# A decoder layer in split fp32: stick-breaking heads started apart, their block sums added before the product, and the first loads and table products spaced out

## The chip, the cores and the metric

The kernel runs on one core of one Trainium2 chip. The metric is the device time of one execution in microseconds (us). The kernel before took 1091.46 us, the median of 3 runs (1091.45 to 1092.46). The profile shows another, single execution, whose own time was 1093.85 us; its instructions span 1092.1 us.

In the profile PE is TensorE's matmul stream, PEld its weight loads, DVE is VectorE, ACT is ScalarE, POOL is GpSimd, and SP is the engine that issues most of the loads.

## What is computed

One layer of a decoder for 512 tokens of width 1024, all in fp32. Its first half is a mixer with three kinds of attention that share one input projection; its second half is an MLP. The part that the change touches most is the stick-breaking attention, 8 heads of width 64:

```
z        = q @ k.T * scale
log_keep = where(s < t, log_sigmoid(-z), 0)          # = -softplus(z)
later    = reverse_cumsum(log_keep, over keys) - log_keep
a        = where(s < t, exp(log_sigmoid(z) + later), 0)
o        = a @ v
```

So the weight of key s for query t needs the sum of softplus(z) over all keys between s and t. The other parts are: differential attention (4 heads, with a bias by distance), dilated attention (12 heads in 3 groups, with a bias by distance), a gated merge and an output projection, a layer norm, then `x <- LN(alpha * x + MLP(x) + sigmoid(x Wg) * (p Wp))`.

## The kernel before

**Split fp32.** An fp32 product is made of three products of rounded halves: a value is cast to a rounded type (`h`, on ACT as a rule), the rest is `lo = x - h` (on DVE), and PE sums `h*h`, `h*lo` and `lo*h` in one PSUM bank. Weights go the same way: a load (512 KB, queue SP) into one of 4 `raw` buffers, an ACT cast to `wh` (L223), a DVE subtraction to `wl` (L224), then the matmuls. A projection item is 24 matmuls of 128 x 512. Where a value is -1 or 0 in the other factor (a matrix of ones or a triangle), two products are enough, one with `h` and one with `lo`.

**Items and steps.** The program is a list of items: two projections together at the start (`first_item`, whose 8 pieces of x and 5 pieces of weights have loads of their own), then one projection or one 128-token piece of V each, then the branch products, the output projection and the MLP. The main loop (from L1280) takes items in order. For each it splits weights ahead (`pump`, L229), evacuates the item before from its PSUM bank (two `mm` banks take turns), calls `step()` and issues the matmuls, with another `step()` in the middle. Attention runs as generators that `step()` (L1261) advances: in `waiting` stand 8 stick-breaking heads, 4 dilated heads and 16 blocks of differential attention. A stick-breaking head counts for 3 PSUM banks of 8, so two run at a time; it is advanced at every second step. The next in line starts when the banks allow it and at least `GAP` = 1 step has gone by. So heads 0 and 1 start one step apart, and later pairs as the pair before ends.

**What the order is.** The text order gives priorities. A scheduler then writes one fixed instruction list for each engine, and an engine works through its list in order. Most tiles come from one pool of 42 SBUF buffers of 128 x 512 fp32 (`slot`, L74); a tile can be written only when a buffer is free. A second pool holds 6 PSUM banks (`at_bank`). `tc.issue_after(i)` puts instructions behind `i` on their own engine.

**A stick-breaking head** (`sb_head`, L968). The keys are 4 blocks of 128, and block kb is needed for the queries from kb on: 512, 384, 256 and 256 columns. Blocks 2 and 3 share a bank (`bi` = 2), blocks 1 and 0 have one each. First come q.k products and masks; then per bank the softplus (three ACT passes, one DVE pass, L991 to L994) into `e`, and its split into `sph` (DVE cast, L997) and `spl` (DVE, L998). Then per key block, from the last to the first, a product with a triangle (`tri_r`, L1008) adds the sum inside the block, and for every later block a product with ones (`ones_r`, L1011) adds that block's whole sum, each twice for `sph` and `spl`. After that come exp, split, and the product with V.

**Tables.** The distance biases come from a one-hot matrix: `tables()` (L899), called at item 13, loads it (three DMAs of the POOL queue), makes five products with the bias table (`rel_vec`, L871, 33 rows by 4 columns), copies each on ACT (L873), writes it to DRAM and reads it back shifted (POOL queue, L882). `turn_tables()` at item 21 reverses them with 8 DVE copies (L892). The dilated heads use them first.

**The start.** Nine matmuls on zeros (L831) run while the first loads come in. `fill()` (L169) issues all loads it can, the first 17 in a fixed order on SP: x piece 0, weights 0, x piece 1, weights 1, x 2, x 3, weights 2 and so on.

**The end.** Output rows are finished 128 at a time. `plain` (L699) adds the last products for `tt` = 0 to 3. For `tt` < 3 the norm is `layer_norm_act` (L463): sums on ACT, a power on POOL (L474), two scaling passes (L476) and two finishing passes (L478) on DVE, then the stores. The last rows come in three pieces with statistics on DVE (L742, L743) and `last_norm` (L752).

## Time and profile before

| | before |
|---|---|
| median of 3 runs | 1091.46 us |
| the profiled execution, its own time | 1093.85 us |
| its span of instructions | 1092.1 us |
| PE busy, share of the span | 99% |
| DVE busy | 62% |
| ACT busy | 44% |
| granted PE clock, mean | 0.997 |
| data moved by DMA | 105.71 MB, 97 GB/s |

A row of the timeline has the start in us from the span's start, the duration in us, the engine, the line, the operation, output <- inputs, the shape, and in square brackets how long the engine had been idle before and what ended that. Matmuls overlap: a row's duration is longer than the distance to the next start, and the distance is what a matmul costs in a dense stream. A row of the groups has the count, the busy time, the mean in ns, then the idle time before and its causes. A row of the windows has, for one stretch, the length and each engine's busy us with the number of instructions, then the granted PE clock, the DMA share and GB/s.

### The profile page before, as it was taken

The numbers are of one execution on the slowest core, as the hardware profiler recorded it, in microseconds if no ns is written. First come the engines' busy times: TensorE is split into PE (matmuls) and PEld (weight loads), VectorE is DVE, ScalarE is ACT, GpSimd is POOL, SyncE is SP. The second block draws the span as 40 slices with busy tenths as digits, with TensorE's granted clock in tenths as the row PEclk, the third lists the DMA queues.
The fourth block names the chain that finished last, engine by engine and source line by source line (L and its number), as shares of the span: only waits on it lengthen the run. The fifth ranks groups of instructions, "written<-read, shape, count | busy, mean of one in ns | idle before, by whom it ended". The sixth has DMA issues, their size and how long they took to land.

```text
span 1092.1 us, 13135 instructions
## 1 busy us (share of the span) xinstructions
PE 1078.9 (99%) x5039; PEld 901.4 (83%) x5039; DVE 674.6 (62%) x1197; ACT 478.4 (44%) x795; POOL 31.0 (3%) x55
## 2 busy tenths in 40 slices
PE   9999999999999999999999999999999999999997
PEld 6788788999888888888888888888888888888885
DVE  5878366564343757665444453875686686687676
ACT  6756354443232546455332331333554454454441
POOL 0000200000000000000000020110000000000000
PEclk9999999999999999999999999999999999999999
DMA  7422421120322113122232253243222422322302
GB/s 250 127 97 85 136 78 58 59 97 21 117 89 83 59 39 107 68 78 87 87 97 101 93 182 127 77 166 108 93 97 78 135 97 77 135 97 79 134 1 77
DMA packets 32431, 105.71 MB, mean 97 GB/s; under 512 B 4378, under 2 KB 5290, under 8 KB 32368
## 3 DMA queue, kind: packets, MB, share of 16 engines
q1 hardware_dynamic: 29424, 96.91, 26.2%
q0 software_dynamic: 2368, 7.05, 2.0%
q8 instruction: 39, 0.64, 0.2%
q10 hardware_dynamic: 576, 0.92, 0.2%
q14 instruction: 24, 0.20, 0.1%
HBM read 102.74 MB, written 2.12 MB: 96 GB/s over the span
## 4 chain that ended last, share of the span: by engine, by line
PE 95%; DVE 3%; DMA 1%; ACT 1%; issue 0%; SPq 0%; POOL 0%; DVEq 0%; ACTq 0%
PE mm L87 17%; PE mm L88 17%; PE mm L89 17%; PE mm L333 3%; PE mm L335 3%; PE mm L334 3%; PE mm L672 2%; PE mm L674 2%; PE mm L673 2%; PE at L672 2%; PE at L674 2%; PE at L673 2%; PE mm L567 1%; PE mm L503 1%; PE mm L501 1%; PE mm L568 1%
## 5 line engine op out<-in xcount | busy, mean ns | idle before, releaser
L223 ACT CAST wh<-raw 128x1024 fp32r<-128x1024 f32 (+1 forms) x173 | 178.3, 1031 | 288.7 <-PE mm L88 229.4
L224 DVE TENSOR_TENSOR wl<-raw,wh 128x1024 fp32r<-128x1024 f32 (+1 forms) x173 | 206.2, 1197 | 123.5 <-ACT wh L223 119.7
L87 PE MATMUL mm<-xhT,wh 128*128 128x512 f32 x496 | 196.5, 396 | 0.0
L89 PE MATMUL mm<-xhT,wl 128*128 128x512 f32 x496 | 194.7, 393 | 0.0
L88 PE MATMUL mm<-xlT,wh 128*128 128x512 f32 x496 | 194.5, 392 | 0.0
L89 PEld LDWEIGHTS mm<-xhT,wl 128*128 128x128 f32 x496 | 93.6, 189 | 19.6
L88 PEld LDWEIGHTS mm<-xlT,wh 128*128 128x128 f32 x496 | 93.6, 189 | 18.3 <-issue 0.4
L87 PEld LDWEIGHTS mm<-xhT,wh 128*128 128x128 f32 x496 | 93.5, 189 | 18.2
L87 PE MATMUL mm<-x1hT,wh 128*128 128x512 f32 x256 | 99.6, 389 | 0.0
L88 PE MATMUL mm<-x1lT,wh 128*128 128x512 f32 x256 | 99.6, 389 | 0.0
L89 PE MATMUL mm<-x1hT,wl 128*128 128x512 f32 x256 | 99.6, 389 | 0.0
L333 PE MATMUL mm<-wh,xhT 128*128 128x512 f32 x160 | 65.6, 410 | 0.6 <-DVE sb_kb L108 0.6
L335 PE MATMUL mm<-wh,xlT 128*128 128x512 f32 x160 | 63.1, 394 | 0.0
L334 PE MATMUL mm<-wl,xhT 128*128 128x512 f32 x160 | 63.0, 394 | 0.0
L89 PEld LDWEIGHTS mm<-x1hT,wl 128*128 128x128 f32 x256 | 48.1, 188 | 10.0
L88 PEld LDWEIGHTS mm<-x1lT,wh 128*128 128x128 f32 x256 | 48.1, 188 | 10.0
L87 PEld LDWEIGHTS mm<-x1hT,wh 128*128 128x128 f32 x256 | 48.1, 188 | 9.9
L223 ACT CAST wh<-wsum 128x1024 fp32r<-128x1024 f32 x28 | 29.5, 1055 | 52.5 <-PE mm L88 49.3
L224 DVE TENSOR_TENSOR wl<-wsum,wh 128x1024 fp32r<-128x1024 f32 x28 | 34.2, 1222 | 24.2 <-ACT wh L223 23.6
L333 PEld LDWEIGHTS mm<-wh,xhT 128*128 128x128 f32 x160 | 38.0, 237 | 4.2 <-issue 0.8
L335 PEld LDWEIGHTS mm<-wh,xlT 128*128 128x128 f32 x160 | 38.0, 237 | 3.9
L334 PEld LDWEIGHTS mm<-wl,xhT 128*128 128x128 f32 x160 | 38.2, 239 | 3.3
(336 smaller groups left out, 1972.7 us busy)
## 6 DMA issues: line engine op xcount, KB each, us to landing
raw<-in_wt_dram SPq DMA_DIRECT2D x62, 512.0 KB, 3.3
raw<-in_wu_dram SPq DMA_DIRECT2D x32, 512.0 KB, 3.3
raw<-in_wd_dram SPq DMA_DIRECT2D x32, 512.0 KB, 3.3
raw<-in_wv_dram SPq DMA_DIRECT2D x20, 512.0 KB, 3.3
raw<-in_wb_dram SPq DMA_DIRECT2D x8, 512.0 KB, 3.4
raw<-in_wo_dram SPq DMA_DIRECT2D x8, 512.0 KB, 3.7
raw<-in_wg_dram SPq DMA_DIRECT2D x8, 512.0 KB, 4.2
rawx<-in_xT_dram SPq DMA_DIRECT2D x8, 256.0 KB, 6.0
```

Of the source, the lines that this page charges most:

```text
L87: nc.tensor.matmul(ps, wh, xh, start=start, stop=False, skip_group_check=True)
L88: nc.tensor.matmul(ps, wh, xl, start=False, stop=False, skip_group_check=True)
L89: nc.tensor.matmul(ps, wl, xh, start=False, stop=stop, skip_group_check=True)
L223: nc.scalar.copy(h, raw)
L224: i = nc.vector.tensor_sub(lo, raw, h.bitcast(F32))
L333: nc.tensor.matmul(ps, x1, c["h"][:, s], start=k == 0, stop=False)
L334: nc.tensor.matmul(ps, x1, c["l"][:, s], start=False, stop=False)
L335: nc.tensor.matmul(ps, x2, c["h"][:, s], start=False, stop=k == 7)
L501: nc.tensor.matmul(ps, h[:, q], c["h"][:, s], start=k == 0, stop=False)
L672: nc.tensor.matmul(ps, h[:, q], c["h"][:, s], start=go, stop=False, skip_group_check=True)
L673: nc.tensor.matmul(ps, h[:, q], c["l"][:, s], start=False, stop=False, skip_group_check=True)
L674: nc.tensor.matmul(ps, lo[:, q], c["h"][:, s], start=False, stop=end, skip_group_check=True)
```

## The change

There are five edits and a small one.

1. **Sums ahead of the split.** In `sb_head`, after the softplus of bank 2 DVE adds the two key blocks' `e` (256 columns) into `sm`, ACT casts it and DVE subtracts (a split of 256 columns). After that of bank 1 DVE adds `sm` to `e` in place, and ACT and DVE split that (384 columns). Each of key blocks 2, 1 and 0 then gets one pair of products with ones, from these summed halves, in place of a pair for every later block.
2. **Heads apart.** `GAP` becomes `gap`, 7 steps (3.5 items) until at most 20 generators wait, which is when the 8 stick-breaking heads have started, and 1 after that.
3. **First loads.** `fill()` issues only 4 loads until the first cast of x is in the program, and load 4 (x piece 2) waits on SP for that cast to be done.
4. **One-hot products.** `rel_vec` and `tables` become generators: each step issues one product with its copy and its store, and the shifted loads come in the step after the last. `turn_tables()` moves from item 21 to 22.
5. **The third norm's end.** `layer_norm_act` returns its two finishing passes as a function. For `tt` = 2 they are issued behind the first addition of the last rows (L742).
6. `pump` may split two chunks, where it was one, at items 0, 1 and 2.

```diff
--- before.py
+++ after.py
@@ -140,9 +140,9 @@
 
 
         RING, RAW, NSUM = 7, 4, 3
-        ORDERED = 17
+        ORDERED, AHEAD = 17, 4
         loads, sums, chunks, placed = [], [], [], []
-        st = {"dma": 0, "sum": 0, "split": 0}
+        st = {"dma": 0, "sum": 0, "split": 0, "most": 4}
 
         def load(src, w, own=False):
             s = {"src": src, "w": w, "uses": 0, "own": own}
@@ -167,7 +167,7 @@
             return chunk_of(load(src, w))
 
         def fill():
-            while st["dma"] < len(loads):
+            while st["dma"] < min(len(loads), st["most"]):
                 s = loads[st["dma"]]
                 if not s["own"]:
                     if len(placed) >= RAW and placed[-RAW]["uses"]:
@@ -184,6 +184,10 @@
                 else:
                     i = nc.sync.dma_start(s["raw"], s["src"])
                 st["load"] = getattr(i, "ins", i)
+                if st["dma"] == AHEAD:
+
+                    tc.add_manual_dep(st["load"], st["cast"].name, mybir.DependencyInfo(
+                        mybir.DependencyClass.Sync, mybir.DependencyReason.DATA), reason="first loads alone")
                 st["dma"] += 1
                 add()
             add()
@@ -220,7 +224,9 @@
                 parts = c["dst"]
             for h, lo, a0, a1 in parts:
                 raw = c["from"]["raw"][:, a0:a1]
-                nc.scalar.copy(h, raw)
+                cast = nc.scalar.copy(h, raw)
+                if st["split"] == 0:
+                    st["cast"], st["most"] = getattr(cast, "ins", cast), 1 << 30
                 i = nc.vector.tensor_sub(lo, raw, h.bitcast(F32))
                 st["low"] = getattr(i, "ins", i)
             c["from"]["uses"] -= 1
@@ -474,9 +480,12 @@
             nc.gpsimd.tensor_tensor(r, r, mhalf, OP.pow)
             for h in range(2):
                 nc.vector.scalar_tensor_tensor(ts[h], ts[h], nmu, lnc[g][h], op0=OP.add, op1=OP.mult)
-            for h in range(2):
-                nc.vector.scalar_tensor_tensor(ts[h], ts[h], r, lnc[b][h], op0=OP.mult, op1=OP.add)
-                fin(h, ts[h])
+
+            def rest():
+                for h in range(2):
+                    nc.vector.scalar_tensor_tensor(ts[h], ts[h], r, lnc[b][h], op0=OP.mult, op1=OP.add)
+                    fin(h, ts[h])
+            return rest
 
         xn = {}
 
@@ -698,7 +707,7 @@
 
             def plain(cs, c2, c3, c4):
 
-                sums = {}
+                sums, held = {}, []
                 s6 = slot("bn6e")[:, :18].rearrange("p (a b) -> p a b", b=6)
 
                 ends = [(0, slice(0, 512)), (1, slice(0, 256)), (1, slice(256, 512))]
@@ -737,9 +746,16 @@
                                 def fin(h, y):
                                     (nc.sync if h else nc.scalar).dma_start(
                                         out[0, tt * P:tt * P + P, 512 * h:512 * h + 512], y)
-                                layer_norm_act([acc[tt, 0], acc[tt, 1]], sums[tt], "ln2_g", "ln2_b", fin)
+                                rest = layer_norm_act([acc[tt, 0], acc[tt, 1]], sums[tt], "ln2_g", "ln2_b", fin)
+                                if tt == 2:
+                                    held.append(rest)
+                                else:
+                                    rest()
                             return
-                        nc.vector.tensor_add(t[:, cc], t[:, cc], ps[:, :n])
+                        i = nc.vector.tensor_add(t[:, cc], t[:, cc], ps[:, :n])
+                        if held:
+                            with tc.issue_after(getattr(i, "ins", i)):
+                                held.pop()()
                         nc.vector.bn_stats(s6[:, ends.index((half, cc)), :], t[:, cc])
                         if (half, cc) == ends[2]:
                             last_norm()
@@ -872,6 +888,7 @@
                 sb = slot("rvs")[0:4, :]
                 nc.scalar.copy(sb[:, :n], ps[0:4, :n])
                 nc.gpsimd.dma_start(rv[cols, d0:d0 + n], sb[:, :n])
+                yield
 
         def shifted(h0, n, m):
             ts = []
@@ -903,10 +920,10 @@
             nc.gpsimd.dma_start(oh[0][:33, :], ohd[:, 0:512])
             nc.gpsimd.dma_start(oh[1][:33, :], ohd[:, 512:1024])
             nc.gpsimd.dma_start(oh[2][:33, :], ohd[:, 1024:1536])
-            rel_vec(slice(0, 4), [(oh[0][:33, :], 0, 512), (oh[1][:33, 0:128], 512, 128)])
-            rel_vec(slice(4, 8), [(oh[1][:33, 128:512], 0, 384)])
-            rel_vec(slice(8, 12), [(oh[2][:33, 0:256], 0, 256)])
-            rel_vec(slice(12, 16), [(oh[2][:33, 256:512], 0, 256)])
+            yield from rel_vec(slice(0, 4), [(oh[0][:33, :], 0, 512), (oh[1][:33, 0:128], 512, 128)])
+            yield from rel_vec(slice(4, 8), [(oh[1][:33, 128:512], 0, 384)])
+            yield from rel_vec(slice(8, 12), [(oh[2][:33, 0:256], 0, 256)])
+            yield from rel_vec(slice(12, 16), [(oh[2][:33, 256:512], 0, 256)])
             tab_g0 = shifted(4, 4, 256)
             tab_g1 = shifted(8, 4, 128)
             tab_g2 = shifted(12, 4, 128)
@@ -983,7 +1000,7 @@
                     nc.tensor.matmul(ps[:, 0:P], identb, mask_b[:, 1, :], start=False, stop=False,
                                      skip_group_check=True)
             w = [512, 384, 512]
-            sph, spl = {}, {}
+            sph, spl, later = {}, {}, {}
             for bi in (2, 1, 0):
                 n = w[bi]
                 ps = bank[bi][:, :n]
@@ -1000,16 +1017,33 @@
 
                     tie[:] = [getattr(i, "ins", i) for i in (ln, low)]
                 sph[bi], spl[bi] = h, lo
+
+                if bi == 2:
+                    later[2] = (256, (h[:, HC], lo[:, HC]))
+                    sm = slot("sm")[:, HB]
+                    nc.vector.tensor_add(sm, e[:, HB], e[:, HC])
+                    hl = slot("smp", F32R)
+                    nc.scalar.copy(hl[:, HB], sm)
+                    nc.vector.tensor_sub(hl[:, HC], sm, hl[:, HB].bitcast(F32))
+                    later[1] = (256, (hl[:, HB], hl[:, HC]))
+                elif bi == 1:
+                    nc.vector.tensor_add(e[:, 128:384], e[:, 128:384], sm)
+                    h = slot("smh", F32R)[:, :n]
+                    lo = slot("sml", F32R)[:, :n]
+                    nc.scalar.copy(h, e)
+                    nc.vector.tensor_sub(lo, e, h.bitcast(F32))
+                    later[0] = (384, (h, lo))
                 yield
             ah, al = {}, {}
             for kb, bi, c0, n in reversed(blk):
                 ps = bank[bi][:, c0:c0 + n]
                 for hl in (sph, spl):
                     nc.tensor.matmul(ps, tri_r, hl[bi][:, c0:c0 + n], start=False, stop=False, skip_group_check=True)
-                for kb2, bi2, d0, n2 in blk[kb + 1:]:
-                    for hl in (sph, spl):
-                        nc.tensor.matmul(bank[bi][:, c0 + n - n2:c0 + n], ones_r, hl[bi2][:, d0:d0 + n2],
-                                         start=False, stop=False, skip_group_check=True)
+                if kb < 3:
+                    n2, hl = later[kb]
+                    for t in hl:
+                        nc.tensor.matmul(bank[bi][:, c0 + n - n2:c0 + n], ones_r, t, start=False, stop=False,
+                                         skip_group_check=True)
                 if kb == 3:
                     continue
                 n = w[bi]
@@ -1254,15 +1288,17 @@
         BANKS = 8
         HALF = True
         last = [-99]
-        GAP = [1]
+        gap = [7]
 
         clock = [0]
 
         def step():
             clock[0] += 1
-            if waiting and sum(e[0] for e in active) + waiting[0][0] <= BANKS and clock[0] - last[0] >= GAP[0]:
+            if waiting and sum(e[0] for e in active) + waiting[0][0] <= BANKS and clock[0] - last[0] >= gap[0]:
                 active.append(waiting.popleft() + (clock[0],))
                 last[0] = clock[0]
+                if len(waiting) <= 20:
+                    gap[0] = 1
             for e in list(active):
                 if (clock[0] - e[3]) % e[2]:
                     continue
@@ -1291,7 +1327,7 @@
             if prev is not None:
                 prev[0]["ev"](prev[1])
 
-            pump(freed, 1 if n < 10 else 2)
+            pump(freed, 1 if 2 < n < 10 else 2)
             if n == 4:
                 tie.clear()
                 with tc.issue_after(st["load"]):
@@ -1300,8 +1336,8 @@
                 with tc.issue_after(st["low"]):
                     make_lam()
             if n == 13:
-                tables()
-            if n == 21:
+                pending.append(tables())
+            if n == 22:
                 turn_tables()
             if n == wout_at - 9:
                 load_pT()
```

## The prediction

> **What bounds the kernel now.** I read the page's busy line and the chain that ended last first, then PE's timeline around the places that the change touches, then DVE's.
>
> ```profile
> PE 1078.9 (99%) x5039; PEld 901.4 (83%) x5039; DVE 674.6 (62%) x1197; ACT 478.4 (44%) x795; POOL 31.0 (3%) x55
> PE 95%; DVE 3%; DMA 1%; ACT 1%; issue 0%; SPq 0%; POOL 0%; DVEq 0%; ACTq 0%
> ```
>
> PE is busy for 99% of the span and carries 95% of the chain. So PE work that goes is worth its full price, as long as no wait takes its place, and work added to DVE or ACT costs nothing where PE stays fed. But busy is not the same as full speed: the rows below show waits and a slow stretch. All sums are made against the profiled execution (its own time 1093.85 us, span 1092.1 us); it lies 2.4 us above the median of the runs, 1091.46 us, from which I subtract the gain, as it is the runs' median that will be compared.
>
> **1. Fewer products with ones.** The first row is from the groups of the first 320 us, the others from PE's timeline at the end of one head's products.
>
> ```profile
> L1011 PE MATMUL at<-sph,ones_r 128*128 128x256 f32 x40 | 10.5, 281 | 0.0
> ```
> ```profile
> 58.16 0.28 PE L1011 MATMUL at<-sph,ones_r 128*128 128x256 f32 x1
> ...
> 58.63 0.39 PE L333 MATMUL mm<-wh,xhT 128*128 128x512 f32 x1
> 58.86 0.40 PE L334 MATMUL mm<-wl,xhT 128*128 128x512 f32 x1
> ```
>
> The row's duration (0.28 us) is a pipelined one. What a product costs is the distance to the next start: four products of 256 columns, one per half for blocks 2 and 3, fill 58.16 to 58.63, 0.118 us each, and one of 512 columns takes 58.63 to 58.86, 0.23 us. Before, each head has five 256-column products with `sph` (the row's 40 over 8 heads: one for key block 2, two for block 1, two for block 0) and five with `spl`. After, two and two are left (blocks 2 and 1); the 384-column pair for block 0 stays. So 6 products a head and 48 in all go: 48 x 0.118 = **5.6 us**. Bounds: 0, if all of it turns into waits, and 5.6.
>
> What it adds is not on PE. These are the rows nearest in shape, from the same groups.
>
> ```profile
> L998 DVE TENSOR_TENSOR spl<-e,sph 128x384 fp32r<-128x384 f32 x8 | 4.5, 559 | 0.3
> ...
> L346 DVE TENSOR_TENSOR sb_v<-mm,sb_v 128x256 fp32r<-128x256 f32 x8 | 3.4, 421 | 1.3 <-ACT sb_v L345 1.3
> ...
> L345 ACT CAST sb_v<-mm 128x256 fp32r<-128x256 f32 x8 | 3.0, 369 | 7.8 <-DVE sb_v L346 5.9 <-PE mm L335 2.0
> ```
>
> DVE gets three passes of 256 columns (0.42 us each) and one of 384 (0.56): 1.8 us a head, 14.6 us in all. ACT gets a cast of 256 (0.37) and one of 384 (taken as 0.5, between 0.37 and the 0.62 us that a 512-column cast takes in a row below): 0.9 us a head, 7 us in all. The cover is DVE's and ACT's free time, in rows quoted under 2. Were the cover gone, the 14.6 us would stand on the path and the edit would lose 9. The chain to a product grows by an addition, a cast and a subtraction (about 1.4 us), but the first product that needs a sum comes at least two steps after its softplus, and a step is some 2.7 us of matmuls (12 x 0.23), so I put it at nothing.
>
> **2. Heads 7 steps apart.** Today heads 0 and 1 start together, while DVE also splits the weights. PE's timeline, and the windows:
>
> ```profile
> 39.50 0.28 PE L1008 MATMUL at<-sph,tri_r 128*128 128x256 f32 x1
> 41.20 0.39 PE L1008 MATMUL at<-spl,tri_r 128*128 128x256 f32 x1 [1.43 <-DVE spl L998]
> ...
> 42.66 0.44 PE L1008 MATMUL at<-spl,tri_r 128*128 128x384 f32 x1 [0.15 <-DVE spl L998]
> ...
> 44.18 0.47 PE L333 MATMUL mm<-wh,xhT 128*128 128x512 f32 x1 [0.60 <-DVE sb_kb L108]
> ```
> ```profile
> 40.00:60.00 20.00, 18.03 (x87) 15.01 (x88) 16.11 (x32) 11.15 (x24) 0.00 (x0) 1.00 0.26 81
> 60.00:80.00 20.00, 20.00 (x99) 16.04 (x98) 14.72 (x27) 12.13 (x19) 0.00 (x0) 1.00 0.39 132
> ```
>
> In the first pair of heads PE waits three times for DVE. The first distance is 1.70 us where a product costs 0.12, a loss of 1.58; with the 0.15 and 0.60 in brackets that is **2.3 us**. DVE is busy 16.1 of 20 us there. The change puts head 1 six steps later, about 16 us, so its softplus leaves this stretch for one where DVE (14.7 of 20) and ACT (12.1 of 20) have room; what comes in is head 0's 1.8 us. What is late next is the two weight splits that edit 6 pulls ahead, but they also serve PE. Bounds: 0 (DVE is as late with one head) to 2.3; nearest are the rows at 60 to 80 us, full of PE work, so I take 2.3. The later pairs show no such waits, so the spacing gains nothing there. By the counts in the code the last stick-breaking head starts 8 steps later, but the second dilated head waits for its projections at item 35 anyway, so nothing behind it moves.
>
> **3. First loads.** The start of the timeline:
>
> ```profile
> 2.66 0.91 SPq L183 DMA_DIRECT2D rawx<-in_xT_dram  x2
> 3.54 0.62 ACT L223 CAST xhT<-rawx 128x512 fp32r<-128x512 f32 x1 [1.45 <-DMA rawx<-in_xT_dram]
> ...
> 6.79 0.67 PE L314 MATMUL at<-xlT,wh 128*128 128x512 f32 x2
> ...
> 7.55 0.62 ACT L223 CAST xhT<-rawx 128x512 fp32r<-128x512 f32 x1 [2.82 <-DMA rawx<-in_xT_dram]
> ...
> 8.92 0.73 PE L314 MATMUL at<-xhT,wh 128*128 128x512 f32 x2 [1.46 <-ACT wh L223]
> ```
>
> PE has done piece 0 at 7.46 and waits 1.46 us for piece 1, whose x landed 4.0 us after piece 0 (casts at 3.54 and 7.55). The new wait stands on SP: x pieces 2 and 3, issued from 2.66 today, can go no sooner than 4.16, when the first cast ends, and every other load stands behind them. If the later loads took bandwidth from pieces 1, the whole 1.46 us goes. If not, nothing goes, and the loads behind are up to 1.5 us later, which costs at most that. Bounds -1.5 to 1.46; I take half of the gain, **0.7 us**, as rows can't tell which.
>
> [...] The trace shows piece 1 late by 4.0 us with later loads in the queue, and can't show whether they were the cause.
>
> **4. One-hot products.** Around them, and the window just behind:
>
> ```profile
> 109.92 2.75 PE L871 MATMUL at<-oh,rel 33*4 33x512 f32 x10
> ...
> 112.60 0.74 PE L88 MATMUL mm<-xlT,wh 128*128 128x512 f32 x1
> ...
> 116.12 0.39 PE L1030 MATMUL at<-ah,sb_v 128*128 128x512 f32 x1
> ```
> ```profile
> 113.00:114.00 1.00, 1.00 (x4) 0.71 (x4) 0.00 (x0) 0.07 (x1) 1.00 (x3) 0.50 0.05 9
> ```
>
> After 2.75 us of products that use 33 x 4 of the array, the granted clock is 0.50: the 8 full matmuls from 112.60 to 116.12 take 3.52 us in place of 8 x 0.23 = 1.8. Spread by one step, a product (0.3 to 0.9 us) has 2.7 us of full matmuls behind it, and I expect no slow stretch: **1.7 us**. The products' own 2.7 us stay. Bounds: 0, or a slow stretch for some of them again, to 1.7. The three one-hot loads, five copies, five stores and eight shifted loads on POOL's queue move with them, the last by some five steps (14 us); the 8 reversing DVE copies move by one item, far ahead of the dilated heads.
>
> **5. The end.** DVE's timeline:
>
> ```profile
> 1081.46 1.42 DVE L478 SCALAR_TENSOR_TENSOR xn<-xn,lr,ln_b 128x512 f32<-128x512 f32 x2 [0.65 <-POOL lr L474]
> 1082.79 1.01 DVE L742 TENSOR_TENSOR xn<-xn,at 128x512 f32<-128x512 f32 x2
> ```
>
> The addition that waits behind these two passes now goes ahead of them, into the 0.65 us in which DVE waits for POOL. Its bank is ready only shortly before 1081.46, so I take 0.1 us, between 0 and 0.65. The order of the rest, and its stores, stay ahead of the last store.
>
> **The sum.** 5.6 + 2.3 + 0.7 + 1.7 + 0.1 = 10.4. From it I take 0.4 for new waits of the kind below: 10 us, **1081.5 us** by the runs' median (1083.8 for an execution like the profiled one).
>
> **The rivals.**
>
> *Only the products go (about 1085.9 us).* The waits of 2 and the clock of 4 come back elsewhere: one head alone can still be late, as the splits fill DVE, and thin products can still lower the clock. For it: 16.1 of 20 us at DVE. Against it: no such wait from 60 to 80 us. 1091.5 - 5.6.
>
> [...]
>
> *The buffers run out (slower).* Each head asks for four more buffers of the pool of 42, and heads that start up to 8 steps later hold their q and k longer, while the dilated projections already fill it. That it is short today shows in DVE's rows:
>
> ```profile
> 202.55 0.43 DVE L997 CAST sph<-e 128x512 fp32r<-128x512 f32 x1 [2.16 <-PE at L1008]
> ...
> 204.82 0.68 DVE L293 COPY dl_k<-mm 128x512 f32<-128x512 f32 x1
> ```
>
> A cast to `sph` waits 2.16 us for a PE product, which can only be the last reader of the buffer it gets, and the evacuation of `dl_k` comes late behind it. Its place would be items 15 to 31, where, counted through the code in its text order, more than 42 buffers would be in use without a pause. An evacuation that comes later than one item's matmuls (24 x 0.23 = 5.5 us) leaves PE without an `mm` bank. It decides from 10 / 17 = 0.6 us an item; at 1 us over 17 items the time is 1091.5 - 10 + 17 = 1098 us. Against it: PE has no idle row today although this wait is there.
>
> *No net effect (about 1091 us).* The work taken from PE comes back as waits for DVE's 14.6 us.
>
> **Chances.** Forecast 0.36; ring order 0.20; only the products 0.29; no net effect 0.06; buffers 0.09. The first three are all faster: 0.85; same 0.06; slower 0.09, where 0.2% (2.2 us) is about what a measurement of this kernel can tell from no change. The low end of the range is every part at its upper bound, 5.6 + 2.3 + 1.46 + 1.7 + 0.65 = 11.7, with some 2 us for waits that the brackets don't show: 1077.5. The high end takes in the products alone with half of them lost again: 1088.5.
>
> **What would show it.** In the changed profile: 16 rows of 256 columns for the products with ones in each half; no PE wait near 40 us; granted clock 1.00 around the one-hot products; piece 1 cast near 5 us if the later loads were the cause, at 7.5 if not; no PE idle between 120 and 250 us. I would be wrong if PE rows there carry brackets naming an evacuation, or if the casts that wait for PE products grow.

## The result, and the profile after

The changed kernel is slower. Its median is 1098.6 us (4 runs, 1097.45 to 1100.13); the kernel before, run beside it, has 1091.45 us (4 runs, 1091.3 to 1092.46). The ratio is 1.0056, with a 95% interval of 1.0041 to 1.0071. That is 4.5 to 7.8 us more, where 10 us less was forecast. The profiled execution took 1099.44 us, with a span of 1097.7 us (before 1092.1) and a mean granted clock of 0.991 (before 0.997).

The changed kernel's busy line and chain of work that ended last, from its page:

```profile
PE 1080.6 (98%) x4991; PEld 897.4 (82%) x4991; DVE 687.2 (63%) x1229; ACT 483.7 (44%) x811; POOL 30.9 (3%) x55
...
PE 93%; DVE 4%; ACT 1%; issue 1%; DVEq 0%; ACTq 0%
```

PE has 48 instructions fewer (4991 against 5039), as the first edit says, and yet is busy 1.7 us longer. DVE's share of the chain has gone from 3% to 4%: work that was to lie beside PE now stands on the path here and there. The products with ones, from the groups of the first 320 us (count, busy us, mean ns, idle time before):

```profile
L1045 PE MATMUL at<-smp,ones_r 128*128 128x256 f32 x16 | 3.4, 298 | 0.0
...
L1045 PE MATMUL at<-sph,ones_r 128*128 128x256 f32 x8 | 2.2, 281 | 0.0
L1045 PE MATMUL at<-spl,ones_r 128*128 128x256 f32 x8 | 2.2, 278 | 0.0
```

32 products of 256 columns are left of 80. So the work of 48 x 0.118 = 5.6 us went, and some 11 us of other time came.

To see where, I took from the starts of all matmuls the distance to the next one and subtracted what a dense stream costs, some 0.23 us per 512 columns (the median distance is 0.227 us in both profiles) and, as an estimate from that, at least 0.06 us for a short product (128/512 of 0.23). What is left is time in which PE waits, runs at half clock (a granted clock of 0.50), or runs short products. By stretch, in us, for the kernel before, the changed kernel and some experiments told below (stretches shift by a few us between kernels; the cut at 38 us keeps the waits of the first pair of heads in one row):

| stretch | before | after | e1 | e4 | e6 | e9 | e10 | e11 | e13 | e14 | e15 |
|---|---|---|---|---|---|---|---|---|---|---|---|
| 0 to 38 | 4.8 | 5.2 | 4.2 | 7.9 | 5.4 | 6.1 | 5.4 | 5.0 | 5.3 | 5.7 | 7.3 |
| 38 to 60 | 3.3 | 4.8 | 9.7 | 0.4 | 7.5 | 0.4 | 4.9 | 0.5 | 4.8 | 0.4 | 0.4 |
| 60 to 100 | 0.4 | 0.6 | 1.2 | 0.3 | 0.8 | 0.3 | 0.4 | 0.5 | 0.4 | 0.3 | 0.3 |
| 100 to 160 | 3.4 | 3.8 | 15.5 | 3.7 | 3.6 | 2.8 | 3.0 | 2.7 | 9.6 | 2.8 | 8.1 |
| 160 to 200 | 0.4 | 0.8 | 6.8 | 0.7 | 0.3 | 0.7 | 0.4 | 0.4 | 0.5 | 0.7 | 0.5 |
| 200 to 260 | 6.7 | 12.6 | 5.6 | 11.0 | 6.8 | 8.8 | 6.4 | 7.3 | 8.8 | 8.7 | 8.3 |
| 260 to the end | 14.9 | 17.6 | 18.6 | 16.7 | 14.8 | 14.3 | 15.5 | 16.5 | 16.1 | 14.2 | 14.9 |
| whole span | 34.1 | 45.6 | 61.8 | 40.9 | 39.3 | 33.5 | 36.2 | 33.1 | 45.8 | 33.0 | 40.0 |

Each column is one profiled execution, which lies up to 2.4 us from the median of its kernel's runs (the kernel before: 1093.85 against 1091.46), so a difference of 1 or 2 us between columns says little.

From before to after the whole is 11.5 us more; minus the 5.6 us of products that makes 5.9, and the span grew by 5.6. The largest part stands at 200 to 260 us (+5.9). Behind 260 us there are 2.7 us more, in pieces of under 0.5 us each. At 38 to 60 us, where edit 2 was to take 2.3 us away, there are 1.5 more.

The waits of PE, grouped by what ended them, in the changed kernel (us in total, times, longest):

```profile
PE mm L339 <- DVE sb_kb L108: 2.9, 1, 2.9
PE at L1064 <- DVE ah L1054: 2.7, 2, 2.2
```

and the largest of them in the kernel before:

```profile
PE at L1008 <- DVE spl L998: 1.6, 2, 1.4
```

The 2.9 us are one wait, at 43.72 us in the timeline of the changed kernel:

```profile
40.09 0.42 DVE L1030 TENSOR_TENSOR e<-e,sm 128x256 f32<-128x256 f32 x1
...
40.39 0.40 PE L1045 MATMUL at<-smp,ones_r 128*128 128x256 f32 x2
40.55 0.51 ACT L1033 CAST smh<-e 128x384 fp32r<-128x384 f32 x1 [3.63 <-DVE e L1030]
40.96 0.59 ACT L115 ACTIVATE sb_ka<-mm 64x512 fp32r<-64x512 f32 x1
...
42.88 0.69 DVE L108 SCALAR_TENSOR_TENSOR sb_kb<-mm,sb_kb 64x512 fp32r<-64x512 f32 x1
...
43.72 0.47 PE L339 MATMUL mm<-wh,xhT 128*128 128x512 f32 x1 [2.93 <-DVE sb_kb L108]
...
47.41 0.43 PE L339 MATMUL mm<-wh,xhT 128*128 128x512 f32 x1
```

ACT stands idle for 3.63 us with the new cast of the sum (L1033) at the head of its list, because DVE adds that sum only at 40.09. Behind the cast in ACT's list are the evacuations of the projection item that has just ended (L115, L116). So its bank is free only when DVE has done `sb_kb`, and PE waits for it. The second cost stands behind the first: the granted clock is 0.50 from 44.06 to 47.47 us, and the nine matmuls from 43.72 to 47.41 take 3.69 us, where nine at 0.2265 us, the distance in the densest stretches, take 2.04. The place is the one where edit 2 was to take waits away.

The second place, in the timeline of the changed kernel:

```profile
222.31 1.22 DVE L230 TENSOR_TENSOR wl<-raw,wh 128x1024 fp32r<-128x1024 f32 x1
...
223.92 0.49 PE L1064 MATMUL at<-ah,sb_v 128*128 128x512 f32 x1 [2.24 <-DVE ah L1054]
224.25 2.50 PE L1164 MATMUL at<-dl_k,dl_q 128*128 128x128 f32 x8
226.79 0.49 ACT L1008 ACTIVATE e<-at 128x384 f32<-128x384 f32 x1 [4.24 <-PE at L1164]
226.79 0.69 DVE L1055 TENSOR_TENSOR al<-a,ah 128x512 fp32r<-128x512 f32 x1 [2.93 <-PE at L1164]
...
230.52 0.51 ACT L1033 CAST smh<-e 128x384 fp32r<-128x384 f32 x1 [2.13 <-DVE e L1030]
230.94 0.58 ACT L96 COPY dl_v<-mm 128x512 f32<-128x512 f32 x1
...
231.57 0.79 PE L87 MATMUL mm<-xhT,wh 128*128 128x512 f32 x1 [0.43 <-ACT dl_v L96]
...
235.15 0.42 PE L89 MATMUL mm<-xhT,wl 128*128 128x512 f32 x1
```

The last stick-breaking heads meet the dilated ones here. PE first waits 2.24 us for `ah` (L1054), which stands behind a weight split (L230) in DVE's list. Then a softplus on ACT (L1008) and a split on DVE (L1055) wait 4.24 and 2.93 us for products of a dilated head (L1164), which compute nothing that they read. What can link them is the pool: they write into buffers, and those products can have been the last to read them. This is argued, not measured, and e4 below shows the same two waits with three of the sums' four buffers gone. Behind that softplus stands the cast of the sum (L1033), for which ACT waits another 2.13 us, and behind the cast the evacuation of `dl_v` (L96), at 230.94 us; only then has PE a bank for the next projection. Until then it has short products alone. The granted clock is 0.50 from about 225 to 235.2 us; it falls behind the wait of 2.24 us and while the short products run, and the rows don't part these two causes. The windows of the changed kernel show both places:

```profile
40.00:60.00 20.00, 17.07 (x70) 13.81 (x69) 11.96 (x25) 9.91 (x21) 0.00 (x0) 0.91 0.21 53
100.00:120.00 20.00, 20.00 (x89) 14.09 (x88) 12.44 (x23) 9.51 (x19) 2.77 (x5) 1.00 0.29 90
...
220.00:240.00 20.00, 16.55 (x66) 13.00 (x65) 11.68 (x23) 8.80 (x15) 0.00 (x0) 0.74 0.30 105
```

And those of the kernel before:

```profile
100.00:120.00 20.00, 20.00 (x92) 15.20 (x91) 7.36 (x12) 4.99 (x10) 9.24 (x16) 0.91 0.35 102
220.00:240.00 20.00, 20.00 (x104) 18.44 (x103) 12.97 (x52) 9.99 (x24) 0.00 (x0) 1.00 0.32 106
```

PE was full from 220 to 240 us; now it is busy for 16.55 of 20 us at a clock of 0.74. Only the one-hot products' stretch has got better: 0.91 before, 1.00 after.

### The profile page after: what moved, and what is told of

It reads as the page before. It is cut to its first block, busy times and chain, and to the rows that moved or that the text cites. A ratio compares the mean times of both kernels' runs of the same rounds, so it can differ in the third digit from the quotient of the medians.

```text
span 1097.7 us, 13110 instructions
## 1 busy us (share of the span) xinstructions
PE 1080.6 (98%) x4991; PEld 897.4 (82%) x4991; DVE 687.2 (63%) x1229; ACT 483.7 (44%) x811; POOL 30.9 (3%) x55
## 4 chain that ended last, share of the span: by engine, by line
PE 93%; DVE 4%; ACT 1%; issue 1%; DVEq 0%; ACTq 0%
PE mm L87 17%; PE mm L89 17%; PE mm L88 17%; PE mm L339 3%; PE mm L341 3%; PE mm L340 3%; PE mm L683 2%; PE mm L681 2%; PE mm L682 2%; PE at L683 2%; PE at L681 2%; PE at L682 2%; PE mm L576 1%; PE mm L578 1%; PE mm L512 1%; PE mm L510 1%
## 5 line engine op out<-in xcount | busy, mean ns | idle before, releaser
L230 DVE TENSOR_TENSOR wl<-raw,wh 128x1024 fp32r<-128x1024 f32 (+1 forms) x173 | 206.3, 1197 | 107.0 <-ACT wh L227 103.0
L89 PE MATMUL mm<-xhT,wl 128*128 128x512 f32 x496 | 194.6, 392 | 0.0
L89 PEld LDWEIGHTS mm<-xhT,wl 128*128 128x128 f32 x496 | 93.5, 189 | 20.8 <-issue 1.1
L89 PE MATMUL mm<-x1hT,wl 128*128 128x512 f32 x256 | 99.6, 389 | 0.0
L89 PEld LDWEIGHTS mm<-x1hT,wl 128*128 128x128 f32 x256 | 48.1, 188 | 10.0
L230 DVE TENSOR_TENSOR wl<-wsum,wh 128x1024 fp32r<-128x1024 f32 x28 | 34.2, 1222 | 24.2 <-ACT wh L227 23.6
```

The lines of the kernel that those rows point to most:

```text
L89: nc.tensor.matmul(ps, wl, xh, start=False, stop=stop, skip_group_check=True)
L230: i = nc.vector.tensor_sub(lo, raw, h.bitcast(F32))
```

## The experiments

My first theory was that the spacing of the heads (edit 2) is the cause, as it moves the last heads into the dilated ones; the rival was that the sums (edit 1) cost more than they save. The first three kernels take these apart.

**e1: the sums alone.** The kernel before with edit 1 and nothing else.

```diff
+                if kb < 3:
+                    n2, hl = later[kb]
...
-        gap = [7]
+        gap = [1]
```

> The kernel before with the summed halves alone (edit 1); heads start one step apart, loads, tables and end as before. Theory A (the loss is the spacing of the heads, which keeps buffers of the pool of 42 in use longer, so that an evacuation and with it PE wait near 221 us): 48 products less and no such wait, about 1086 us. Theory B (the sums themselves cost: 14.6 us more DVE work and four more buffers a head): 1091 us or more, with PE idle rows between 120 and 250 us.

Measured: 1114.07 us, ratio 1.0184 (1.0159 to 1.0209). Alone the sums cost about 20 us. PE's waits in e1:

```profile
PE at L1041 <- DVE sph L1014: 8.8, 4, 2.9
PE at L1064 <- DVE ah L1054: 3.4, 1, 3.4
```

**e2: the spacing alone.** The kernel before with edit 2 and nothing else.

```diff
-        GAP = [1]
+        gap = [7]
...
+                if len(waiting) <= 20:
+                    gap[0] = 1
```

> The kernel before with the heads 7 steps apart alone (edit 2). Theory A: slower than before, 1093 to 1098 us, with a PE wait near 220 us, if the spacing alone fills the pool; 1090 to 1092 us if it takes the sums' four buffers as well. Theory B: not slower, about 1089 us.

Measured: 1095.64 us, ratio 1.0027 (1.0014 to 1.0041). It costs some 3 us, not the 6 that the changed kernel loses by its ratio.

**e3: all but the spacing.** The changed kernel with `gap = [1]`.

```diff
-        gap = [7]
+        gap = [1]
```

> The changed kernel with the heads one step apart again; all other edits stay. Theory A: the waits near 42 us and 221 us go, 1082 to 1086 us. Theory B: still above 1091 us.

Measured: 1114.71 us, ratio 1.0193 (1.0173 to 1.0212). So the theory falls: without the spacing the change is some 15 us worse. The sums are the cause, and the spacing hides most of what they cost (which part of the spacing does so is seen in e13).

**Why the sums cost.** (What e4 was expected to do was written before the results of e1 to e3.) They ask for four more pool buffers a head and put two round trips from DVE to ACT and back into lists that are worked in order. Two mends tell these apart. In the first the sum of blocks 2 and 3 is written in place into `e`, and the halves of the second sum lie in a ring for partial sums that is idle in this phase; one pool buffer of the four is left. In the second the casts of the sums go to DVE, so that there is no round trip.

**e4: the whole change, sums in the idle ring.**

```diff
-                    sm = slot("sm")[:, HB]
+                    sm = e[:, HB]
...
-                    h = slot("smh", F32R)[:, :n]
-                    lo = slot("sml", F32R)[:, :n]
+                    r = ring.tile([P, 1024], F32R, name=nm("smhl"), tag="wsum", bufs=NSUM)
+                    h, lo = r[:, :n], r[:, 512:512 + n]
```

> The changed kernel, heads still 7 steps apart, but the sum is made in place in e and the split of 384 columns goes into the weight-sum buffers, which idle until the MLP: three of the four added buffers of the pool are not asked for. Theory A with the pool of 42 as the cause: the wait near 221 us goes or shrinks, 1088 to 1092 us (the wait near 42 us stays). If the spacing costs in another way, or theory B: 1096 to 1100 us as before.

Measured: 1093.28 us, ratio 1.0000 (0.9987 to 1.0013). By the ratios some 6 us come back. The loss at 38 to 60 us is gone (0.4 in the table), though 0 to 38 us has 2.7 us more than in the changed kernel; that at 200 to 260 us is nearly all there (11.0). This is the other way round from what I expected. From e4's timeline:

```profile
224.63 0.49 ACT L1008 ACTIVATE e<-at 128x384 f32<-128x384 f32 x1 [4.59 <-PE at L1164]
224.63 0.69 DVE L1055 TENSOR_TENSOR al<-a,ah 128x512 fp32r<-128x512 f32 x1 [3.29 <-PE at L1164]
```

So the waits for the products of the dilated head are not made by the three buffers that e4 does without.

**e5: the sums alone, casts on DVE.** e1 with this:

```diff
-                    nc.scalar.copy(hl[:, HB], sm)
+                    nc.vector.tensor_copy(hl[:, HB], sm)
...
-                    nc.scalar.copy(h, e)
+                    nc.vector.tensor_copy(h, e)
```

> The sums alone as in e1 (1114 us), but both new casts on DVE in place of ACT, so that no chain goes from DVE to ACT and back. Theory C (in e1 ACT waits in order for DVE's sum, up to 3.5 us, with the next bank's softplus behind it, and DVE then waits for ACT's cast): 1092 to 1102 us; DVE has 0.6 us a head more to do. Theory A' (four more buffers of the pool of 42 are what costs): still about 1112 us.

Measured: 1105.47 us, ratio 1.0122 (1.0106 to 1.0137). Some 7 of e1's 20 us go with the round trip, less than theory C said and more than theory A' allowed.

**e6: the sums alone, in the idle ring.** e1 with the diff of e4.

> The sums alone as in e1, casts on ACT, but the sum in place in e and the 384-column split in the weight-sum buffers that idle until the MLP: three pool buffers less. Theory A': the waits go, 1086 to 1094 us. Theory C: still 1106 to 1114 us.

Measured: 1094.25 us, ratio 1.0019 (1.0010 to 1.0028). Of e1's 20 us, all but two are gone, with the same operations on the same engines: what differs is where the sums lie. What is left stands at the first pair of heads (7.5 us in 38 to 60, against 3.3 before), where PE's waits in e6 name DVE:

```profile
PE at L1041 <- DVE sph L1014: 2.5, 1, 2.5
```

**e7: the sums alone, both mends,** and **e8: the whole change, both mends.**

> The sums alone with both mends, casts on DVE and three pool buffers less. If A' and C hold together: the 5.6 us of the 48 products show, 1086 to 1088 us. If the 14.6 us of DVE work cost by themselves (theory B): 1095 us or more.

> The whole change with both mends. e4 (buffers alone) gave 1093.3 us. Theory C: the casts on DVE save something more, 1086 to 1091 us. Theory A' alone: 1093 us as e4.

Measured: e7 1097.88 us, ratio 1.0052 (1.0037 to 1.0067); e8 1094.63 us, ratio 1.0022 (1.0012 to 1.0032). With the buffers relieved, the casts on DVE make it slower (by the ratios, e7 against e6 by 3.6 us and e8 against e4 by 2.4). The round trip to ACT is not the main cost. At 38 to 60 us e7, which has no round trip, still loses 6.5 us by the reckoning of the table.

**e9: sums in the ring, only the first pair apart.** e4 with the spacing ended as soon as head 1 has started.

```diff
-                if len(waiting) <= 20:
+                if len(waiting) <= 26:
                     gap[0] = 1
```

> The whole change with the sums in the idle ring (three pool buffers fewer a head, as in e4), and the spacing of seven steps kept for the first two heads alone; all later heads start one step apart, as in the kernel before. Theory (short buffers make the sums dear, the spacing of the later heads moves the last ones into the dilated heads at 200 to 240 us, and the first pair is the only place that gains from spacing): e4's loss at 40 to 60 us stays away, e4's losses at 218.9 and 224.0 us go, and the time is 1093.3 less some 6 to 8 us: 1085.5 to 1087.5 us. Rival (any spacing costs, because the order of the engines' lists shifts for all that follows): 1092 to 1095, with a stall at some new place after 100 us.

Measured: 1087.87 us, ratio 0.9956 (0.9939 to 0.9974): faster than both kernels, and just above the theory's range. From e9's timeline:

```profile
35.20 0.47 PE L339 MATMUL mm<-wh,xhT 128*128 128x512 f32 x1 [1.30 <-DVE sb_qlb L108]
35.50 0.40 PE L340 MATMUL mm<-wl,xhT 128*128 128x512 f32 x1
35.74 0.39 PE L341 MATMUL mm<-wh,xlT 128*128 128x512 f32 x1
...
37.07 0.58 ACT L115 ACTIVATE sb_ka<-mm 64x512 fp32r<-64x512 f32 x1
...
37.65 0.59 ACT L116 ACTIVATE sb_kb<-mm 64x512 fp32r<-64x512 f32 x1
...
40.30 0.52 ACT L1033 CAST smhl<-e 128x384 fp32r<-128x384 f32 x1 [1.42 <-DVE e L1030]
```

The evacuations now stand ahead of the sum's cast in ACT's list, and PE no longer waits for them. (The first three rows are told of at the end.) The whole of the table is 33.5 us, as before the change (34.1), so between these two executions the 5.6 us of the products are a gain in full; by the ratio of all runs e9 gains 4.8 us (2.8 to 6.7).

**e10: loads, tables and end alone.** The kernel before with edits 3, 4 and 5.

```diff
-        gap = [7]
+        gap = [1]
...
-            pump(freed, 1 if 2 < n < 10 else 2)
+            pump(freed, 1 if n < 10 else 2)
```

and the products of the kernel before.

> The kernel before with the held loads, the spread one-hot products and the moved end alone: no sums, no spacing, the weight splits at the old rate. Theory: these are worth what the prediction gave them, 0.7 + 1.7 + 0.1 = 2.5 us, so 1089 us; the granted clock is 1.00 at 100 to 120 us. Rival (they too bring waits of their own): 1091 to 1093.

Measured: 1094.14 us, ratio 1.0013 (1.0000 to 1.0026), so not my 1089; by the ratio it is some 1.4 us slower, as the rival allowed. From e10's timeline:

```profile
39.51 1.05 ACT L227 CAST wh<-raw 128x1024 fp32r<-128x1024 f32 x1 [2.11 <-DMA raw<-in_wt_dram]
...
40.59 1.23 DVE L230 TENSOR_TENSOR wl<-raw,wh 128x1024 fp32r<-128x1024 f32 x1 [0.91 <-ACT wh L227]
...
42.48 0.38 PE L1026 MATMUL at<-spl,tri_r 128*128 128x256 f32 x1 [2.06 <-DVE spl L1015]
```

A weight load is late, DVE's list has the weight split ahead of `spl`, and PE waits 2.06 us, with half clock behind it (from 44.01 to 47.43 us; the granted clock is 0.91 from 40 to 60 us): 4.9 us in 38 to 60 against 3.3. The gain of 100 to 160 us, 0.4, is less than that, and 0 to 38 us shows none (5.4 against 4.8).

**e11: no sums.** The changed kernel with the products of the kernel before; edits 2 to 6 stay.

```diff
-                if kb < 3:
-                    n2, hl = later[kb]
...
+                for kb2, bi2, d0, n2 in blk[kb + 1:]:
```

> The changed kernel with the products of the kernel before in place of the sums; spacing, loads, one-hot products, end and splits stay. Theory (the spacing's loss of about 4 us in e2 is there also without the sums, less the 2.5 us of the other edits): 1092 to 1094 us; the stalls at 220 to 240 us are as in e2 or a little more. Rival (spacing costs only because the sums' buffers come with it): 1087 to 1089.

Measured: 1093.07 us, ratio 1.0008 (0.9998 to 1.0018), as the theory said: edits 2 to 6 together bring nothing. But 200 to 260 us costs 7.3, little more than before (6.7), so most of the changed kernel's loss there (12.6) comes only with the sums.

**e12: e9 with the old rate of weight splits** (edit 6 undone).

```diff
-            pump(freed, 1 if 2 < n < 10 else 2)
+            pump(freed, 1 if n < 10 else 2)
```

> The kernel of e9 with the weight splits at their old rate in the first three items (edit 6 undone). If the earlier splits matter for the first pair of heads: over 1 us slower than e9, with waits at 18 to 47 us. If they are neutral: within 1 us of e9.

Measured: 1089.02 us, ratio 0.9971 (0.9961 to 0.9982). It is 1.2 us above e9, and its stretch from 38 to 60 us has 1.2 us more lost time. The intervals of the ratios overlap, but every run of e12 (1088.59 to 1089.85) lies above every run of e9 (1087.38 to 1088.22), so the earlier splits are worth about a microsecond here.

**e13: e9 with the sums in the pool,** as the change has them.

```diff
-                    sm = e[:, HB]
+                    sm = slot("sm")[:, HB]
...
-                    r = ring.tile([P, 1024], F32R, name=nm("smhl"), tag="wsum", bufs=NSUM)
-                    h, lo = r[:, :n], r[:, 512:512 + n]
+                    h = slot("smh", F32R)[:, :n]
+                    lo = slot("sml", F32R)[:, :n]
```

> The changed kernel with the spacing of seven steps kept for the first pair of heads alone, and the sums in the pool as in the change (so it differs from e9 by where the sums lie, from the changed kernel by the later heads' spacing). Theory (the pool's buffers are what the sums cost, and the later spacing hides part of it): clearly slower than e9 and slower than the changed kernel, 1100 to 1112 us, with PE stalls between 100 and 140 us behind late casts. Rival (the first pair's spacing alone repairs the sums, wherever they lie): within 2 us of e9's 1087.9.

Measured: 1100.33 us, ratio 1.0069 (1.0047 to 1.0090), at the low end of what the theory said. e9 and e13 differ only in where the sums lie, and by 0.0113 in the ratio, some 12 us. That e13 is slower than the changed kernel, as the theory also said, is not shown: the intervals overlap. But e3, which differs from e13 in the first pair's spacing alone, is slower than it by 0.0124, some 13.5 us. So it is the spacing of the first pair that hides most of the sums' cost, and not that of the later heads. The stall behind 120 us, from e13's timeline:

```profile
121.22 0.63 ACT L1010 ACTIVATE e<-e 128x512 f32<-128x512 f32 x1
...
122.39 1.23 DVE L230 TENSOR_TENSOR wl<-raw,wh 128x1024 fp32r<-128x1024 f32 x1 [6.08 <-PE mm L89]
...
124.25 0.43 DVE L1014 CAST sph<-e 128x512 fp32r<-128x512 f32 x1
...
124.73 0.51 PE L1041 MATMUL at<-sph,tri_r 128*128 128x512 f32 x1 [2.44 <-DVE sph L1014]
```

DVE is idle for 6.08 us with a weight split at the head of its list; the softplus behind it could have gone on at 121.85, and PE runs out of work meanwhile. The split waits for products of a projection (L89), which read earlier halves of weights, so not for a buffer of the pool. If the pool makes itself felt here, it is through the order of the lists; how, the row doesn't show.

**e14: e9 without the held loads** (edit 3 undone).

```diff
-        st = {"dma": 0, "sum": 0, "split": 0, "most": 4}
+        st = {"dma": 0, "sum": 0, "split": 0, "most": 1 << 30}
...
-                if st["dma"] == AHEAD:
+                if False:
```

> The kernel of e9 without the held first loads (edit 3 undone). If the later loads delay piece 1 of x: piece 1 is cast at about 7.5 us again as in the kernel before, PE waits some 1.5 us for it, and the time is 0.5 to 1.5 us above e9. [...]

Measured: 1086.72 us, ratio 0.9943 (0.9928 to 0.9958), the fastest of all kernels here, 4.6 to 7.9 us under the kernel before. Piece 1 of x in e9's timeline:

```profile
5.97 0.62 ACT L227 CAST xhT<-rawx 128x512 fp32r<-128x512 f32 x1 [1.39 <-DMA rawx<-in_xT_dram]
```

and in e14's:

```profile
7.26 0.62 ACT L227 CAST xhT<-rawx 128x512 fp32r<-128x512 f32 x1 [2.04 <-DMA rawx<-in_xT_dram]
```

So holding the later loads back does bring piece 1 earlier, by 1.3 us. But PE's wait there is ended by the cast of the weights that come with it, and is 0.87 us in e9 and 1.12 us in e14; and up to 38 us e14 has lost 5.7 us and e9 6.1. Nothing of the gain is left, and e9 is not the faster one.

**e15: e9 with the one-hot products in one go** (edit 4 undone).

```diff
-                pending.append(tables())
-            if n == 22:
+                [None for _ in tables()]
+            if n == 21:
```

> The kernel of e9 with the one-hot products in one go, as in the kernel before (edit 4 undone). Theory: a stretch at a granted clock of 0.50 behind them, and 1 to 2 us more than e9. Rival: no change within 0.5 us.

Measured: 1093.74 us, ratio 1.0007 (0.9997 to 1.0017), by the ratios some 5.6 us above e9. That is more than the theory said, and not by its cause. From e15's timeline:

```profile
114.93 0.59 PE L887 MATMUL at<-oh,rel 33*4 33x256 f32 x2
115.45 0.50 PE L89 MATMUL mm<-xhT,wl 128*128 128x512 f32 x1
...
120.31 1.23 DVE L230 TENSOR_TENSOR wl<-raw,wh 128x1024 fp32r<-128x1024 f32 x1 [8.70 <-ACT wh L227]
...
122.79 0.49 PE L1064 MATMUL at<-ah,sb_v 128*128 128x512 f32 x1 [2.78 <-DVE ah L1054]
```

The scheduler put full matmuls between the one-hot products all the same, and there is no slow stretch behind them (the granted clock is 1.00 from 100 to 120 us). The cost is a new stall at 122.79 us, again with a weight split ahead of a head's pass in DVE's list.

## Why the prediction was wrong, point by point

**Step 1, the products (5.6 us): the saving is right, "I put it at nothing" failed.** 48 products went, and e9 shows their 5.6 us as a gain. What failed is the price of the additions. I counted DVE's and ACT's time (14.6 and 7 us), found room for it in shares of busy time, and took the chain of 1.4 us as covered by two steps. The runs show some 26 us in its place when the sums stand alone in the pool (the 20 us of e1 and the 5.6 that it should have gained), and 18 of e1's 20 us go when three of the four buffers do (e6). The round trip, which I had in view, is the smaller part (some 7 us, e5). At the first pair of heads the sums cost even in the ring: e6 loses 7.5 us there against 3.3, and e7, without the round trip, 6.5. In the changed kernel itself two things add up by the ratios: where the sums lie is worth some 6 us (e4 against the changed kernel), and with the sums in the ring the later heads' spacing some 5 us more (e9 against e4).

**Step 2, the heads apart (2.3 us): right at the first pair, wrong behind it.** In e11, without the sums, the stretch from 38 to 60 us costs 0.5 us in place of 3.3, and e9 has 0.4: about what the forecast took away. But alone the spacing costs some 3 us (e2), so the gain is lost elsewhere. In the changed kernel that stretch costs 4.8, as the sum's cast stands ahead of the evacuations in ACT's list. "Nothing behind it moves" failed too: the late last heads meet the dilated ones, and e4, which differs from e9 only in the later heads' spacing, is slower by 0.0044 in the ratio, some 5 us. That head 1 would come 16 us later was read from the text order. Its first q.k product in the kernel before:

```profile
26.44 0.36 PE L138 MATMUL at<-sb_qb,sb_kb 128*128 128x256 f32 x1
```

and in the changed kernel:

```profile
32.29 0.28 PE L138 MATMUL at<-sb_qb,sb_kb 128*128 128x256 f32 x1
```

It moved by 5.9 us: the lists are made from priorities and from what is ready, and six steps of text are not six steps of time.

**Step 3, the first loads (0.7 us): the effect on piece 1 right, the worth nothing.** In the changed kernel piece 1 was cast here:

```profile
5.99 0.62 ACT L227 CAST xhT<-rawx 128x512 fp32r<-128x512 f32 x1 [1.22 <-DMA rawx<-in_xT_dram]
```

The kernel before cast it at 7.55 us, and e9 and e14 show the same difference by itself (5.97 and 7.26 us): with later loads in the queue piece 1 comes 1.3 to 1.6 us later. So the case that the chances call "ring order", in which piece 1 lands as late as before, is not borne out in either pair. By what means the later loads delay it was not shown. The step that failed is "I take half of the gain": the other bound, loads behind that come later, takes it back by 38 us. e10 shows how. PE no longer waits for piece 1 (1.46 us before), but for the x pieces behind it, which are cast at 9.54 us in place of 8.90:

```profile
10.21 0.73 PE L320 MATMUL at<-xhT,wh 128*128 128x512 f32 x2 [1.13 <-ACT xhT L227]
```

**Step 4, the one-hot products (1.7 us): right as to the clock.** It is 1.00 from 100 to 120 us where it was 0.91. In the changed kernel:

```profile
112.96 1.24 PE L887 MATMUL at<-oh,rel 33*4 33x512 f32 x4
...
116.34 0.50 PE L89 MATMUL mm<-xhT,wl 128*128 128x512 f32 x1
```

The stretch from 100 to 120 us has 1.1 us less of lost time than before. That another order there can cost some 5.6 us (e15) was not in the forecast.

**Step 5, the end (0.1 us): right within what can be seen.** The last matmul starts at 1083.83 us in the kernel before and at 1089.70 us in the changed kernel. From there to the end of the span it is 8.3 us before and 8.0 after.

**The rivals.** "The buffers run out" came true in sign and near in size: 1098 was its figure, and 1098.6 was measured. The nearness is luck, as the lateness is not one of 1 us an item over 17 items. Its witness was the cast that waited 2.16 us for a product before; what I said would show it, passes that wait longer for products, is there with 4.24 us (a softplus) and 2.93 us (a subtraction), though e4 has both too. A PE row that names an evacuation is there with 0.43 us (L96). The lateness stands at two places in the main: at 200 to 260 us, where such waits come on top of lists that have a weight split or a late sum ahead of what PE needs, and at 38 to 60 us, where ACT's list had a late sum ahead of the evacuations. The other three rivals that the chances name, which forecast a gain or no change, fall. I held PE's lack of idle rows before against the rival. That was the wrong row to ask: the question was not whether PE waits now, but how many buffers are free where four more are asked for.

**What stays open.** Why the lists come out in another order when the sums lie in the pool was not measured: the scheduler's own reckoning can't be seen in a trace. e6, e9 and e13 show only that the place of the sums decides it. In them the sum in place and the idle ring come together, and the runs do not part the two. A larger pool, which would ask directly whether buffers were short, was not run. Why the later heads' spacing costs 5 us with the sums in the ring (e4 against e9) and nothing that can be told with the sums in the pool (the changed kernel against e13) is open too.

## What to carry to other kernels

Work that goes to an engine with free time still needs buffers, and it takes a place in a list that is worked in order. So before an addition is put at nothing, count the free buffers at that place, and read what stands behind the new instruction on its engine. Where the lists come from a scheduler, an edit is worth what its new order is worth: edits forecast at 0.1 to 1.7 us each gained nothing together (e10), and a change of three lines, of where a result lies, was worth some 12 us (e9 against e13).

## What the hardware showed that was not expected

A wait of PE can cost more than its length. Behind waits of 2.06 us (e10), 2.78 us (e15) and 2.93 us (changed kernel) there is a stretch of about 3.4 us at a granted clock of 0.50 (from 44.01 to 47.43 us in e10, from 44.06 to 47.47 us in the changed kernel); behind the 1.30 us of e9 at 35.20 us there is none, as the next starts, 0.24 us apart, show. The changed kernel lost 2.93 us in the wait at 43.72 us and 3.69 - 2.04 = 1.65 us behind it. The length alone does not decide, as this row of e1 shows; the granted clock behind it is 1.00, and from 223.45 us on the starts are 0.23 to 0.24 us apart:

```profile
223.11 0.50 PE L1041 MATMUL at<-sph,tri_r 128*128 128x512 f32 x1 [2.19 <-DVE sph L1014]
```

Four slow stretches of e1 begin at 41.87, 110.14, 137.44 and 168.16 us. The distances between them are 68.27, 27.30 and 30.72 us, which are 20, 8 and 9 times 3.413 us. In the changed kernel the slow stretch at 44.06 us is 3.41 us long and that at 224.96 us 10.24 us, three times as long, and their starts are 180.91 us apart, 53 times 3.413 us. So in these two executions the clock changed at whole multiples of about 3.41 us. What makes it fall behind one wait and not behind another was not shown.
